# Moving the split of the first weight sum, and the two adding DMAs behind it, from the second product of a projection into the first

## The chip, the cores and the metric

The kernel runs on one core of a Trainium2 chip. A core has five engines that work side by side, each through its own instruction queue in order: TensorE (PE in the profile; its weight loads are listed as PEld) multiplies matrices, VectorE (DVE) and ScalarE (ACT) do elementwise work, GpSimd (POOL) and SyncE (SP) here mostly issue DMAs. Engines and DMAs wait for each other through semaphores. The metric is the time of one execution on the device in microseconds; a median over several executions is compared with that of another kernel.

## The reference

The reference is one decoder block on x of 1024 tokens by 1024 channels, in float32. What matters here is the middle of it:

```python
merged = (g_pool * jnp.einsum('bsc,cd->bsd', y_pool, w_branch_pool[l])
          + g_attn * jnp.einsum('bsc,cd->bsd', y_attn, w_branch_attn[l]))
mix = jnp.einsum('bsd,de->bse', merged, w_out[l])
x = x + _rmsnorm(mix, g_mix_post[l])
h2 = _rmsnorm(x, g_mlp_pre[l])
```

Before it stand a pooling branch, a windowed attention and two gates; after it a squared-ReLU MLP of 1024 to 4096 to 1024 channels and one more norm. The projection `merged @ w_out`, 1024 x 1024 by 1024 x 1024, is the part that the change touches.

## The kernel before, in words

**Precision.** Every float32 operand of a matmul is split into a high part (a cast to float32r on ScalarE, line 101) and a low part (the source minus the high part, on VectorE, line 104). A product is the sum of three matmul passes (high·high, high·low, low·high, the tuple `PASSES`).

**The projection.** It is computed as a 2 x 2 block product with seven block products instead of eight, each of 512 x 512 by 512 x 512. The four blocks of `w_out` are B11, B12, B21 and B22. The order of the products on TensorE is written out by hand: A11·B11, A12·B21 (into the same banks), S1·Q1, S2·Q2, S4·B22, S3·Q3, A22·Q4. S1 to S4 are sums of blocks of the activations. The weight sums are Q1 = B11 + B12, Q2 = Q1 + B22, Q4 = Q2 + B21 and Q3 = B12 + B22. Signs are arranged elsewhere so that only additions are needed.

**How the weight sums are made.** Q1, Q2 and Q4 live one after the other in the same buffers, `q1[0]` and `q1[1]` (128 x 1024 values each, 512 KB; two tiles of rows to each). SyncE loads B11 into them. Then GpSimd issues DMAs that read another block from DRAM and add it to what is in the buffer (`wo_add`, line 1000). Between two additions the current sum has to be split into its own high and low tiles (`wo_split`, which calls the helper of lines 101 and 104), since the next addition overwrites it. So the chain for each half is: add B12, split Q1, add B22, split Q2, add B21, split Q4. Q3 has buffers of its own (`q3`), with one addition. In the profile these buffers are named qr, the split tiles Q1h and Q1l, Q2h and Q2l and so on.

**How the order is set.** In this stage the order on TensorE, VectorE, ScalarE and GpSimd is that of the program text (`tc.manual_schedule`). `wo_mm` is a generator: it issues the 12 matmuls of one row tile (line 1089) and yields; the body of the loop around it then writes the work that follows that step, such as the copy of the finished bank on ScalarE. A product has four steps, 48 matmuls. The adding DMAs go through GpSimd's queue in program order: first two for q3, then two for q1 (B22), two for q1 (B21), and then those that accumulate output halves (line 1274) and write rows to DRAM (line 1127). SyncE's queue carries the plain loads: the weight blocks of the projection (line 995), the first weights of the MLP (line 483) and the rows of x for the residual (line 1120).

**The steps around the change.** In the first product, steps 0 and 1 split the two halves of B21, and each step copies its bank (line 1235 before the change). Between the first and second product the activation sums S1 and S2 are split (`s12`, named gr in the profile). In the second product each step copies its bank (line 1250) and adds an activation block (line 980), and steps 0 and 1 split Q1 and issue the addition of B22. After it B22 is split. In S1·Q1 each step copies its bank (line 1259); steps 0 and 1 split Q2 and issue the addition of B21. Behind the projection the finished rows are normed, added to x (lines 1123 and 1126), and transposed on TensorE (line 1135) for the MLP; some of these transposes stand between the matmuls of the last product.

Of the kernel before, what the change touches and what calls it, by code (L numbers as in the profile page):

```python
# [50 lines left out]
def block_kernel(ctx: ExitStack, tc, xt, x, consts, vecs, sinks, b_qkv, g_post, g_mlp, g_mlp_post,  # L51
# [16 lines left out]
    def nm(s):  # L68
        cnt[0] += 1
        return f"{s}_{cnt[0]}"  # L70
# [16 lines left out]
    def bank(tag, shape=None):  # L87
        return psum["pool"].tile([P] + (shape or [512]), F32, tag=tag, name=nm(tag), bufs=psum["bufs"][tag])
# [4 lines left out]
    def flat(t):  # L93
        return t.rearrange("p a b -> p (a b)")
# [4 lines left out]
    def split(hi, lo, src, eng=dve, first=None):  # L99
        if first is None:  # L100
            act.copy(hi, src)  # L101
        else:
            first.tensor_copy(hi, src)
        eng.tensor_tensor(lo, src, f32(hi), ALU.subtract)  # L104
# [732 lines left out]
    def gr(shape):  # L837
        return gp.tile([P] + shape, F32R, tag="g", name=nm("gr"))
# [116 lines left out]
    def flip(dst, src):  # L955
        act.activation(dst, src, AF.Identity, scale=-1.0)

    def split_half(tile_, src):
        t = tile_([2, 512])
        split(t[:, 0, :], t[:, 1, :], src)  # L960
        return t[:, 0, :], t[:, 1, :]

    def merged(m):
        zp = zm[m]
        first, second = zp[:, :512], zp[:, 512:]
        if m < 4:
            if m % 2 == 0:
                s3raw.append(ga_.tile([P, 2, 512], F32, tag="ga", name=nm("s3")))
            Am["A11"][m] = split_half(gr, first)
            dve.tensor_tensor(s3raw[m // 2][:, m % 2, :], first, second, ALU.subtract)  # L970
        else:
            k = m - 4
            s2, s1 = zm[k][:, :512], zm[k][:, 512:]
            Am["A12"][k] = split_half(ar, first)
            dve.tensor_tensor(s1, second, s1, ALU.subtract)
            dve.tensor_tensor(s2, s2, s1, ALU.add)

    def sum4(k):
        first = zm[4 + k][:, :512]
        dve.tensor_tensor(first, zm[k][:, :512], first, ALU.subtract)  # L980

    def wo_rows(c, h, j):
        return w_o[4 * h + 2 * c:4 * h + 2 * c + 2].rearrange("k p n -> p k n")[:, :, 512 * j:512 * j + 512]

    def wo_split(name, c, src, tile_):
        hi, lo = tile_(name + "h"), tile_(name + "l")
        split(hi, lo, flat(src))
        Wm.setdefault(name, [None] * 4)
        for i in range(2):
            Wm[name][2 * c + i] = hi[:, i * 512:(i + 1) * 512], lo[:, i * 512:(i + 1) * 512]  # L990

    def wo_raw(name, c, tile_):
        h, j = {"B11": (0, 0), "B12": (0, 1), "B21": (1, 0), "B22": (1, 1)}[name]
        t = tile_([2, 512])
        nc.sync.dma_start(t, wo_rows(c, h, j))
        return t

    def wo_add(t, name, c):
        h, j = {"B11": (0, 0), "B12": (0, 1), "B21": (1, 0), "B22": (1, 1)}[name]
        nc.gpsimd.dma_start(t, wo_rows(c, h, j), accum_op=ALU.add)  # L1000
# [18 lines left out]
    def bp_mul(m):  # L1019
        zp = gate_of.pop(m)  # L1020
        for th in range(2):
            sl = slice(th * 512, (th + 1) * 512)
            dve.tensor_tensor(zp[:, sl], zp[:, sl], bs_of[m][th], ALU.mult)
        dve.tensor_tensor(zp, zp, za[m], ALU.add)
        zm.append(zp)
# [4 lines left out]
    with tc.manual_schedule(engines=MANUAL):  # L1030
        q1 = [wo_raw("B11", c, wraw) for c in range(2)]
# [53 lines left out]
    def wo_mm(bs, a, w, after=False):  # L1085
        for t in range(4):
            for k in range(4):
                for j, (ah, wh) in enumerate(PASSES):
                    pe.matmul(bs[t], Am[a][k][ah][:, t * P:(t + 1) * P], Wm[w][k][wh],  # L1089
                              start=not after and k == 0 and j == 0, stop=k == 3 and j == 2, skip_group_check=after)  # L1090
            yield t
# [6 lines left out]
    def out_sq(n, h):  # L1098
        act.activation(junk_b[:, :512], ct[n][:, h * 512:(h + 1) * 512], AF.Square, scale=ROOT_D,
                       accum_out=osq[:, h, n:n + 1])  # L1100
# [121 lines left out]
    with tc.manual_schedule(engines=MANUAL):  # L1222
        bp_mul(7)
        bm = [bank("mm") for _ in range(4)]
        merged(7)
        q3 = [wo_raw("B12", c, wraw) for c in range(2)]
        for c in range(2):
            wo_add(q3[c], "B22", c)
        for t in wo_mm(bm, "A11", "B11"):
            if t == 0:  # L1230
                wo_split("B21", 0, b21[0], wo_tile)
            elif t == 1:
                wo_split("B21", 1, b21[1], wo_tile)
            ct[4 + t] = xq.tile([P, D], F32, tag="x1", name=nm("c2"))
            act.copy(ct[4 + t][:, :512], bm[t])
        flip(gpost_b[:, 512:], gpost_b[:, 512:])

        def s12(k):
            hi, lo = gr([D]), gr([D])
            split(hi, lo, zm[k])  # L1240
            Am["S2"][k] = hi[:, :512], lo[:, :512]
            Am["S1"][k] = hi[:, 512:], lo[:, 512:]

        b22 = [wo_raw("B22", c, stage) for c in range(2)]
        for k in range(4):
            s12(k)
        up.load(0)
        for t in wo_mm(bm, "A12", "B21", True):
            ct[t] = yy.tile([P, D], F32, tag="y", name=nm("c1"))
            act.copy(ct[t][:, :512], bm[t])  # L1250
            if t < 2:
                wo_split("Q1", t, q1[t], wo_tile)
                wo_add(q1[t], "B22", t)
            sum4(t)
        for c in range(2):
            wo_split("B22", c, b22[c], wo_tile)
        ba = [bank("at") for _ in range(4)]
        for t in wo_mm(ba, "S1", "Q1"):
            act.copy(ct[4 + t][:, 512:], ba[t])
            Am["A22"][t] = split_half(ar, zm[4 + t][:, 512:])  # L1260
            if t < 2:
                wo_split("Q2", t, q1[t], wo_tile)
                wo_add(q1[t], "B21", t)
            else:
                for k in (2 * t - 4, 2 * t - 3):
                    Am["S4"][k] = split_half(gr, zm[4 + k][:, :512])
        up.operand(0, 1)
        up.operand(0, 2)
        up.load(2)
        bm = [bank("mm") for _ in range(4)]  # L1270
        for t in wo_mm(bm, "S2", "Q2"):
            u = ct[4 + t]
            dve.tensor_tensor(u[:, :512], u[:, :512], bm[t], ALU.subtract)
            nc.gpsimd.dma_start(u[:, 512:], u[:, :512], accum_op=ALU.add)
            out_sq(t, 0)
            Am["S3"][t] = split_half(gr, s3raw[t // 2][:, t % 2, :])
            if t > 1:
                wo_split("Q3", t - 2, q3[t - 2], wo_tile)
# [478 lines left out]
```

## Time and profile before

| | us |
|---|---|
| median of 3 runs | 1108.01 |
| lowest and highest run | 1105.50 and 1108.25 |
| the profiled execution, its own time | 1107.79 |
| span of the profiled execution | 1106.0 |
| TensorE busy | 1095.2 (99% of the span) |
| VectorE busy | 822.8 (74%) |
| ScalarE busy | 551.8 (50%) |
| GpSimd busy | 54.2 (5%) |
| mean granted TensorE clock | 0.997 of full speed |

The projection lies between about 402 and 485 us of the span. Busy time of TensorE includes matmuls that run at a lower granted clock, so a share of 99% does not say that it runs at its fastest. A row of the timeline gives start, duration, engine, line, operation, output and inputs, and in square brackets the idle time of that engine before it and what ended it. Matmuls of 128 x 512 are pipelined: each has a duration of 0.39 us, but at full clock one starts every 0.227 us. Buffer numbers are left out of the names.

### The profile page before, as it was taken

Reading aid. Unit: us, or ns where it says so; the run is one execution under the profiler, and the core shown is the slowest. Engines: PE = TensorE matmul, PEld = TensorE weight load, DVE = VectorE, ACT = ScalarE, POOL = GpSimd, SP = SyncE. Lnnn points to the kernel's source line nnn. Section 1 sums busy time; section 2 is a strip of 40 time slices with the busy share of each in tenths; the row PEclk is TensorE's granted clock in tenths of the full one; section 3 lists DMA queues with packets and bytes.
Section 4 is the critical chain, followed back from the end, with each engine's and each line's share of the span. In section 5 each row is a group of like instructions: output and inputs, shape, how many; then the busy total and the mean of one; then the engine's idle time right before and its main releaser. Section 6 shows DMA issues by size and latency. Waiting matters only on the chain.

```text
span 1106.0 us, 13829 instructions
## 1 busy us (share of the span) xinstructions
PE 1095.2 (99%) x5114; PEld 909.4 (82%) x5114; DVE 822.8 (74%) x1179; ACT 551.8 (50%) x911; POOL 54.2 (5%) x112
## 2 busy tenths in 40 slices
PE   9999999999999999999999999999999999999997
PEld 8888888888888887888888888888888888888886
DVE  6568877898859777988978875756546875447797
ACT  7566665444332236566544544444436535435462
POOL 0334100000000001200000000000000000000000
PEclk9999999999999999999999999999999999999999
DMA  9614466365976564922455553435797876332652
GB/s 347 163 39 155 153 187 232 132 217 196 270 252 205 174 189 97 302 98 100 154 212 212 179 190 109 187 124 200 247 370 266 303 258 197 100 95 71 226 183 91
DMA packets 90803, 206.86 MB, mean 187 GB/s; under 512 B 9328, under 2 KB 22256, under 8 KB 90736
## 3 DMA queue, kind: packets, MB, share of 16 engines
q1 hardware_dynamic: 81072, 176.75, 47.6%
q10 hardware_dynamic: 5760, 19.79, 4.7%
q0 software_dynamic: 3904, 9.44, 3.8%
q8 instruction: 40, 0.66, 0.2%
q14 instruction: 27, 0.22, 0.1%
HBM read 149.32 MB, written 55.58 MB: 185 GB/s over the span
## 4 chain that ended last, share of the span: by engine, by line
PE 92%; DVE 3%; issue 2%; ACT 1%; DMA 1%; POOL 0%; DVEq 0%; POOLq 0%; ACTq 0%
PE mm L520 26%; PE at L520 16%; PE at L1525 15%; PE mm L1525 12%; PE mm L456 4%; PE mm L610 3%; PE mm L1089 3%; PE mm L458 2%; PE mm L192 2%; PE sc L183 2%; PE mm L183 2%; PE sc L429 1%; PE sc L360 1%; PE at L1089 1%; DMA qr<-in_w_o_dram 1%
## 5 line engine op out<-in xcount | busy, mean ns | idle before, releaser
L1525 PE MATMUL at<-ar,wh 128*128 128x512 f32 x696 | 158.7, 389 | 0.0
L1525 PEld LDWEIGHTS at<-ar,wh 128*128 128x128 f32 x696 | 130.6, 188 | 27.1
L1525 PE MATMUL mm<-ar,wh 128*128 128x512 f32 x576 | 131.0, 389 | 0.0
L1525 PEld LDWEIGHTS mm<-ar,wh 128*128 128x128 f32 x576 | 108.1, 188 | 22.5
L104 DVE TENSOR_TENSOR wh<-raw,wh 128x1024 fp32r<-128x1024 f32 x51 | 62.4, 1224 | 79.5 <-ACT wh L101 77.0
L101 ACT CAST wh<-st 128x512 fp32r<-128x512 f32 (+1 forms) x104 | 65.7, 641 | 95.6 <-DVE st L499 24.5
L101 ACT CAST wh<-raw 128x1024 fp32r<-128x1024 f32 x51 | 53.7, 1052 | 112.0 <-PE at L1525 55.4
L104 DVE TENSOR_TENSOR wh<-st,wh 128x512 fp32r<-128x512 f32 (+1 forms) x105 | 74.6, 720 | 30.2 <-ACT wh L101 27.6
L520 PE MATMUL mm<-gr,wh 128*128 128x512 f32 x333 | 79.4, 391 | 0.0
L520 PEld LDWEIGHTS mm<-gr,wh 128*128 128x128 f32 x333 | 62.1, 188 | 12.7
L520 PE MATMUL mm<-T,wx 128*128 128x512 f32 x288 | 67.4, 389 | 0.0
L520 PEld LDWEIGHTS mm<-T,wx 128*128 128x128 f32 x288 | 54.1, 188 | 11.2
L520 PE MATMUL at<-T,wx 128*128 128x512 f32 x252 | 58.9, 389 | 0.0
L520 PEld LDWEIGHTS at<-T,wx 128*128 128x128 f32 x252 | 47.3, 188 | 9.8
L520 PE MATMUL mm<-x,wh 128*128 128x512 f32 x240 | 55.2, 389 | 0.0
L520 PEld LDWEIGHTS mm<-x,wh 128*128 128x128 f32 x240 | 45.1, 188 | 9.3
L104 DVE TENSOR_TENSOR ar<-B,ar 128x1024 fp32r<-128x1024 f32 x37 | 45.2, 1221 | 5.6 <-ACT ar L101 5.5
L610 PE MATMUL mm<-x,wh 128*128 128x512 f32 x192 | 47.7, 395 | 0.0
L101 ACT CAST ar<-B 128x1024 fp32r<-128x1024 f32 x37 | 38.9, 1051 | 7.6 <-DMA B<-in_w_dn_dram 4.6
L610 PEld LDWEIGHTS mm<-x,wh 128*128 128x128 f32 x192 | 35.2, 188 | 7.5 <-DVE qt L104 0.2
L520 PE MATMUL at<-gr,wh 128*128 128x512 f32 x150 | 36.6, 390 | 0.0
L520 PE MATMUL mm<-T,wh 128*128 128x512 f32 x147 | 36.1, 389 | 0.0
(433 smaller groups left out, 2202.4 us busy)
## 6 DMA issues: line engine op xcount, KB each, us to landing
raw<-f_dram SPq DMA_DIRECT2D x53, 512.0 KB, 3.7
f_dram<-g SPq DMA_DIRECT2D x28, 512.0 KB, 3.0
st<-in_w_up_dram SPq DMA_DIRECT2D x24, 512.0 KB, 4.3
B<-in_w_dn_dram SPq DMA_DIRECT2D x24, 512.0 KB, 6.7
st<-in_w_g_dram SPq DMA_DIRECT2D x18, 512.0 KB, 3.9
f_dram<-g ACTq DMA_DIRECT2D x17, 512.0 KB, 3.4
g<-spill_dram SPq DMA_DIRECT2D x16, 512.0 KB, 4.9
raw<-in_w_dn_dram SPq DMA_DIRECT2D x16, 512.0 KB, 4.6
```

Of the source, the lines that this page charges most:

```text
L101: act.copy(hi, src)
L104: eng.tensor_tensor(lo, src, f32(hi), ALU.subtract)
L183: pe.matmul(bq, xs_[k][n // 4][:, xh, n % 4 * P:(n % 4 + 1) * P], wq[k][:, h, :], start=k == 0 and j == 0, stop=k == NK - 1 and j == 2)
L192: pe.matmul(bkv_of(n), xs_[k][n // 4][:, xh, n % 4 * P:(n % 4 + 1) * P], wkv[k // 2][:, h, k % 2, :], start=k == 0 and j == 0 and not (joi ...
L360: pe.matmul(sb[:, kv, i, :nk], qt[r, qx, m * P:(m + 1) * P], kx[r, k0:k0 + nk], start=j == 0, stop=j == 2)
L429: pe.matmul(yb[:, kv], v[:, c:c + P], p[ph][:, 4 * kv:4 * kv + 4].rearrange("p i q -> p (i q)"), start=j < 2, stop=j >= len(mms) - 2)
L456: pe.matmul(bs[th], whi[:, k, :], rhs(k, hl, th), start=k == 0 and hl == 0, stop=False)
L458: pe.matmul(bs[th], wlo[:, k, :], rhs(k, 0, th), start=False, stop=k == nk - 1)
L520: pe.matmul(b, w[:, wh, kt, :], x_, start=not after and kt == 0 and j == 0, stop=kt == 3 and j == 2, skip_group_check=after)
L610: pe.matmul(b, (whi, wlo)[h][:, k, :], xr(k, xh, th), start=j == 0, stop=j == len(mms) - 1)
L1089: pe.matmul(bs[t], Am[a][k][ah][:, t * P:(t + 1) * P], Wm[w][k][wh], start=not after and k == 0 and j == 0, stop=k == 3 and j == 2, skip_g ...
L1525: pe.matmul(bs[t], fo[fh][:, k2, t * P:(t + 1) * P], wo_[wh][:, k2, :], start=not after and s2 == 0 and k2 == 0 and j == 0, stop=(s2, k2) ...
```

## The change

The splits of Q1 move from steps 0 and 1 of the second product into steps 2 and 3 of the first one, ahead of the copy of the bank in those steps. The additions of B22 into q1 move with them and are issued directly behind each split. On GpSimd's queue the order of the DMAs stays; on ScalarE and VectorE the two casts and the two subtractions now stand ahead of the splits of S1 and S2. The instructions themselves stay the same.

```diff
--- before
+++ after
@@ -1231,6 +1231,9 @@
                 wo_split("B21", 0, b21[0], wo_tile)
             elif t == 1:
                 wo_split("B21", 1, b21[1], wo_tile)
+            else:
+                wo_split("Q1", t - 2, q1[t - 2], wo_tile)
+                wo_add(q1[t - 2], "B22", t - 2)
             ct[4 + t] = xq.tile([P, D], F32, tag="x1", name=nm("c2"))
             act.copy(ct[4 + t][:, :512], bm[t])
         flip(gpost_b[:, 512:], gpost_b[:, 512:])
@@ -1248,9 +1251,6 @@
         for t in wo_mm(bm, "A12", "B21", True):
             ct[t] = yy.tile([P, D], F32, tag="y", name=nm("c1"))
             act.copy(ct[t][:, :512], bm[t])
-            if t < 2:
-                wo_split("Q1", t, q1[t], wo_tile)
-                wo_add(q1[t], "B22", t)
             sum4(t)
         for c in range(2):
             wo_split("B22", c, b22[c], wo_tile)
```

## The prediction

> **What bounds the kernel now.** I read the chain of work that ended last, the waits of TensorE, then the order in time of each engine around the changed lines. The chain (shares of the span, by engine), the list of TensorE's waits, and one row of the chain in order of time:
>
> ```profile
> PE 92%; DVE 3%; issue 2%; ACT 1%; DMA 1%; POOL 0%; DVEq 0%; POOLq 0%; ACTq 0%
> ```
>
> ```profile
> PE mm L201 <- DVE pad L160: 1.1, 1, 1.1
> PE mm L1089 <- ACT Q2h L101: 1.0, 1, 1.0
> PE mm L1089 <- DVE Q2l L104: 0.8, 1, 0.8
> PE sc L403 <- DVE s L369: 0.5, 1, 0.5
> ```
>
> ```profile
> 449.46 10.88 PE at L1089 x48
> ```
>
> TensorE is the bound nearly everywhere, so only a change in its own gaps moves the end. These four waits are its whole list (total, times, longest), and two of them lie in the product S2·Q2, which this change is about. An undisturbed product of the projection is 48 matmuls in 10.88 us, 0.2267 us each. The product S2·Q2 starts at 434.43 and the product after it (operand B22) at 449.30 (start, duration, engine, line, operation):
>
> ```profile
> 434.43 0.39 PE L1089 MATMUL mm<-Q2h,gr 128*128 128x512 f32 x1
> ...
> 435.56 0.39 PE L1089 MATMUL mm<-Q2h,gr 128*128 128x512 f32 x1
> 436.98 0.50 PE L1089 MATMUL mm<-Q2h,gr 128*128 128x512 f32 x1 [1.02 <-ACT Q2h L101]
> 438.24 0.50 PE L1089 MATMUL mm<-Q2l,gr 128*128 128x512 f32 x1 [0.76 <-DVE Q2l L104]
> ...
> 449.30 0.39 PE L1089 MATMUL at<-B22h,gr 128*128 128x512 f32 x1
> ```
>
> That is 14.87 us, 3.99 us more than 10.88. The parts: the seventh matmul is due at 435.56 + 0.23 = 435.79 and comes at 436.98 (1.19 lost); the next is due at 437.21 and comes at 438.24 (1.03 lost); the remaining 1.77 us are lost after the waits, where the granted clock is down. The windows show this (length, then busy times of PE, PEld, DVE, ACT, POOL; then granted clock, DMA share, GB/s); the second row is the stretch around the 0.5 us wait of line 403:
>
> ```profile
> 439.30:442.90 3.60, 3.60 (x11) 2.79 (x10) 3.58 (x7) 3.60 (x9) 0.60 (x1) 0.53 0.56 100
> 112.00:116.00 4.00, 3.47 (x22) 2.85 (x21) 3.97 (x7) 1.73 (x4) 0.00 (x0) 1.00 0.99 291
> ```
>
> Eleven matmuls in 3.60 us at clock 0.53, where 16 would fit. A wait of 0.5 us elsewhere left the clock at 1.00; the two of S2·Q2 did not.
>
> **Why S2·Q2 waits.** Its second half of weights is q1[1] after the adding DMA of B22. GpSimd's queue of adding DMAs, and the time from issue to landing of the pair at 401 and 407, of the one at 427.13 and of the one at 442.30:
>
> ```profile
> 401.19 1.21 POOL L1000 DMA_DIRECT2D qr<-in_w_o_dram  x1 [39.82 <-DVE g L1024]
> 407.20 1.22 POOL L1000 DMA_DIRECT2D qr<-in_w_o_dram  x1 [4.81 <-issue]
> 421.13 1.21 POOL L1000 DMA_DIRECT2D qr<-in_w_o_dram  x1 [12.71 <-DVE Q1l L104]
> 427.13 1.21 POOL L1000 DMA_DIRECT2D qr<-in_w_o_dram  x1 [4.79 <-DMA qr<-in_w_o_dram]
> 436.12 1.21 POOL L1000 DMA_DIRECT2D qr<-in_w_o_dram  x1 [7.77 <-DMA qr<-in_w_o_dram]
> 442.30 1.22 POOL L1000 DMA_DIRECT2D qr<-in_w_o_dram  x1 [4.98 <-DVE gr L104]
> ```
>
> ```profile
> qr<-in_w_o_dram POOLq DMA_DIRECT2D x2, 512.0 KB, 5.8
> qr<-in_w_o_dram POOLq DMA_DIRECT2D x1, 512.0 KB, 8.7
> qr<-in_w_o_dram POOLq DMA_DIRECT2D x1, 512.0 KB, 9.1
> ```
>
> In these rows a second adding DMA of 512 KB never starts before the first has landed: the one of 421.13 is followed at 427.13, the one of 427.13 lands at 435.8 and is followed at 436.12. So a pair takes 6 us plus its second landing. The pair of Q2 starts at 421.13 because that is when the first low half of Q1 has been read (released by DVE Q1l). It ends at 435.8, 0.01 us after the seventh matmul was due, and cast (1.04) and subtraction (1.23) are still to come.
>
> **The change, part by part.** It moves two casts on ScalarE, two subtractions on VectorE and two adding DMAs of GpSimd from the second product into the third and fourth steps of the first; nothing is added or removed, and on SyncE's queue and on TensorE the order stays. ScalarE and VectorE before:
>
> ```profile
> 408.57 0.58 ACT L1235 COPY c<-mm 128x512 f32<-128x512 f32 x1
> 410.15 0.59 ACT L1235 COPY c<-mm 128x512 f32<-128x512 f32 x1 [1.00 <-PE mm L1089]
> 412.87 0.59 ACT L1235 COPY c<-mm 128x512 f32<-128x512 f32 x1 [2.13 <-PE mm L1089]
> ...
> 418.14 1.06 ACT L101 CAST Q1h<-qr 128x1024 fp32r<-128x1024 f32 x1
> ...
> 429.67 0.62 ACT L101 CAST ar<-g 128x512 fp32r<-128x512 f32 x1
> 435.88 1.04 ACT L101 CAST Q2h<-qr 128x1024 fp32r<-128x1024 f32 x1 [5.58 <-DMA qr<-in_w_o_dram]
> ```
>
> ```profile
> 408.26 2.36 DVE L104 TENSOR_TENSOR B21l<-st,B21h 128x1024 fp32r<-128x1024 f32 x2
> 414.95 4.63 DVE L104 TENSOR_TENSOR gr<-g,gr 128x1024 fp32r<-128x1024 f32 x4 [4.34 <-ACT gr L101]
> ...
> 436.96 1.23 DVE L104 TENSOR_TENSOR Q2l<-qr,Q2h 128x1024 fp32r<-128x1024 f32 x1 [5.94 <-ACT Q2h L101]
> ...
> 469.42 2.48 DVE L1126 SCALAR_TENSOR_TENSOR c<-g,r,c 128x1024 f32<-128x1024 f32 x2
> ```
>
> *Casts.* ScalarE stands idle 1.00 and 2.13 us ahead of the third and fourth copy. Two casts of 1.06 fit: 409.1 to 410.2, the third copy at 410.2 instead of 410.15, the second cast 410.7 to 411.8, the fourth copy unmoved at 412.87. The banks copied late are rewritten by the second product only at its third and fourth step, over 5 us later. Cost 0. If q1 were not there yet, ScalarE would stop in front of two copies and of the S1/S2 casts; but GpSimd was idle for 39.82 us before its add of 401.19, so the adds of B12 into q1 went out before 362.
>
> *Subtractions.* VectorE idles 4.34 us before 414.95; two of about 1.22 (the row of Q2l has the same shape) run from 410.6 to about 413.0. Cost 0. The casts and subtractions taken out of the second product leave holes there, worth nothing, since the copies around them wait for TensorE.
>
> *Adding DMAs.* They stand behind the q3 pair. Its second, of 407.20, lands at about 413.0, so the first of ours starts at 413.3 rather than at 411.8, where its own data would allow it. At 5.8 it lands at 419.1, at 9.1 at 422.4; the second starts 0.3 later and lands between 425.2 and 431.8. I take 426, near the short end, because the loads of SyncE that come next are these:
>
> ```profile
> 426.62 1.46 SPq L483 DMA_DIRECT2D st<-in_w_up_dram  x2
> ```
>
> The slow add of 427.13 ran beside them; ours are through or nearly so. The second cast of Q2 then follows the cast of 429.67 at 430.3, ends at 431.4, its subtraction at 432.6. TensorE wants them at 435.79 and 436.02. The margin is 3.4 us, and 1.8 us if the add lands at the late end. What is queued behind on GpSimd, the pair of B21 for Q4, goes out at about 430 instead of 436.12, and the adds of the output halves after it come earlier too.
>
> *Sum.* Both waits go (−1.19, −1.03). With no gap left there is nothing in the rows to bring the clock down, so −1.77 goes as well: −3.99 us. ScalarE and VectorE were held by the same DMA (5.58 and 5.94 us idle); without it they reach the work behind no later than the last result of S1·Q1, ready at about 434.6 when TensorE ends that product, so they keep up with it. The list of waits has nothing of TensorE's behind S2·Q2, and the loads there go to slots that come free with the shifted work; the shift reaches the end. Next in line is the first transpose of the normed rows:
>
> ```profile
> 473.79 1.03 PE L1135 MATMUL at<-cst,c 128*128 128x128 f32 x8
> ```
>
> The rows it reads are finished by the VectorE pair of 469.42, at 471.9: a margin of 1.9 us, which has to move along.
>
> The profiled execution took 1107.79 us for a span of 1106.0; 1107.79 − 3.99 = 1103.80. The median of the runs, 1108.01, is 0.22 above the profiled one, so the forecast stands about 4.2 us, 0.38%, under it.
>
> **The rivals.**
> *Only the waits go* (1107.79 − 2.22 = 1105.6). The slow clock could have come from something else than these gaps and stay. Against it: the window of 112 to 116 and the undisturbed products beside it run at 1.00, and the slow stretch begins 1 us after the second gap. For it: neither gap was longer than 1.2 us. The Trainium skill, TensorE: Matmul & The Clock Gate, Part 1, says that the clock is halved after at least one idle window of about 3.4 us; by that rule two gaps of 1.19 and 1.03 would not have done it, and this rival would hold. The trace has the half clock right behind them all the same. Chance 0.07.
>
> *The add lands late all the same; the change does nothing.* Were all of the three adds from 407.20 on to take 9.1 us, the last would land at 407.2 + 3 × 9.1 + 0.6 = 435.1, 0.7 us before now, and the time would be 1107.1. Of the landings above, one reached 9.1, one 8.7, and the pair that stands first in this queue took 5.8. Chance 0.04.
>
> *Given back at the transposes.* If the normed rows stay at 471.9 because their loads of x or VectorE's own chain do not move, TensorE, 4 us ahead at 469.8, waits 2.1 us: 1105.9, and with the clock falling again for 1.77, 1107.7. Against it: VectorE is worked through without a long wait from 437 on. Chance 0.08.
>
> *Slower, at the same place.* If an adding DMA or load of another 8.7 us gets in front of the x loads of these rows, because the GpSimd pair for Q4 and the SyncE loads of 426.62 now overlap, the rows come 8.7 us late: TensorE waits 8.7 − 1.9 = 6.8, plus 1.77 of clock, less 3.99: 1112.4. It decides from rows later than about 4.1 us against before. Against it: the Q4 pair, from 430 on, is then out of the way by 430 + 6.0 + 9.1 = 445, where now it lands at 442.3 + 9.1 = 451.4. Chance 0.07.
>
> **How the numbers follow.** The forecast has 0.74. A difference of 0.3% is 3.3 us, about what a measurement of this kernel tells from no change; the three runs alone lie 2.75 us apart, so 0.05 of the 0.74 may still measure less. Faster: 0.69. Within: 0.05 + 0.07 + 0.04 + 0.08 = 0.24. Slower: 0.07. The lower end of the range is the lowest run, 1105.5, less 3.99: 1101.5; the upper end takes in the late add and most of the given-back case, 1107.1.
>
> **What would show it.** The changed profile should have: the casts of Q1h near 409 and 411; adds issued near 413 and 419; no wait of TensorE for Q2h or Q2l; S2·Q2 in 10.88 us, clock 1.00; the B21 add near 430; the first transpose near 469.8 with no wait ahead of it. I am wrong if the second Q2 add lands after 433, if the slow clock shows up with no gap before it, or if TensorE waits at line 1135.

## The result, and the profile after

| | before | after |
|---|---|---|
| median, us (10 runs each, side by side) | 1108.12 | 1104.14 |
| lowest and highest, us | 1105.50 and 1109.08 | 1103.57 and 1105.36 |
| profiled execution: time and span, us | 1107.79 and 1106.0 | 1104.10 and 1102.3 |
| mean granted TensorE clock | 0.997 | 0.998 |

The ratio is 0.997, with a 95% interval of 0.996 to 0.998: faster by 0.3%, 3.98 us between the medians. The forecast was 1103.8.

The chain of the profile after, as shares by engine, and the whole list of TensorE's waits (total, times, longest):

```profile
PE 97%; DVE 2%; ACT 1%; issue 0%; DVEq 0%; ACTq 0%
```

```profile
PE mm L201 <- DVE pad L160: 1.1, 1, 1.1
PE sc L403 <- DVE s L369: 0.5, 1, 0.5
```

The DMA's 1% and the 2% of issue time are gone from the chain: before, it ran back from the wait for Q2 through GpSimd's queue, now it stays on TensorE there. These shares are not time saved. Both waits for Q2 are gone from the list. The chain in order of time (start, duration, what) shows S2·Q2, in the banks named mm, and the B22 product behind it; then the window of S2·Q2 (length, busy times of PE, PEld, DVE, ACT, POOL, then the granted clock, DMA share, GB/s):

```profile
434.57 10.88 PE mm L1089 x48
445.45 10.88 PE at L1089 x48
```

```profile
434.20:445.10 10.90, 10.90 (x50) 9.03 (x49) 8.64 (x14) 9.62 (x20) 3.85 (x4) 1.00 0.75 162
```

S2·Q2 takes 10.88 us at clock 1.00. The B22 product stood at 449.46 in the chain before and stands at 445.45 now: 4.01 us earlier. GpSimd's queue after (start, duration, engine, line, operation, and the idle time before it), then the landing times of the two that feed Q2:

```profile
402.06 1.21 POOL L1000 DMA_DIRECT2D qr<-in_w_o_dram  x1 [42.08 <-PE mm L458]
407.97 1.22 POOL L1000 DMA_DIRECT2D qr<-in_w_o_dram  x1 [4.71 <-PE mm L1089]
414.17 1.21 POOL L1000 DMA_DIRECT2D qr<-in_w_o_dram  x1 [4.98 <-issue]
420.06 1.21 POOL L1000 DMA_DIRECT2D qr<-in_w_o_dram  x1 [4.68 <-DMA qr<-in_w_o_dram]
430.18 1.21 POOL L1000 DMA_DIRECT2D qr<-in_w_o_dram  x1 [8.90 <-DVE Q2l L104]
436.39 1.22 POOL L1000 DMA_DIRECT2D qr<-in_w_o_dram  x1 [5.00 <-issue]
```

```profile
qr<-in_w_o_dram POOLq DMA_DIRECT2D x1, 512.0 KB, 5.6
qr<-in_w_o_dram POOLq DMA_DIRECT2D x1, 512.0 KB, 5.9
```

The pair for Q2 now follows the q3 pair at the pitch of this queue, about 6 us, and the second of it has landed at 420.06 + 5.9 = 426.0, before SyncE's loads of 426.6 begin. Before, it was issued at 427.13. ScalarE and VectorE:

```profile
409.01 1.06 ACT L101 CAST Q1h<-qr 128x1024 fp32r<-128x1024 f32 x1
410.13 0.59 ACT L1238 COPY c<-mm 128x512 f32<-128x512 f32 x1
410.61 1.05 ACT L101 CAST Q1h<-qr 128x1024 fp32r<-128x1024 f32 x1
412.85 0.59 ACT L1238 COPY c<-mm 128x512 f32<-128x512 f32 x1 [1.18 <-PE mm L1089]
...
430.17 1.05 ACT L101 CAST Q2h<-qr 128x1024 fp32r<-128x1024 f32 x1
```

```profile
410.49 2.43 DVE L104 TENSOR_TENSOR Q1l<-qr,Q1h 128x1024 fp32r<-128x1024 f32 x2
414.93 4.63 DVE L104 TENSOR_TENSOR gr<-g,gr 128x1024 fp32r<-128x1024 f32 x4 [2.01 <-ACT gr L101]
...
431.25 1.23 DVE L104 TENSOR_TENSOR Q2l<-qr,Q2h 128x1024 fp32r<-128x1024 f32 x1 [0.26 <-ACT Q2h L101]
465.40 2.48 DVE L1126 SCALAR_TENSOR_TENSOR c<-g,r,c 128x1024 f32<-128x1024 f32 x2
```

```profile
469.77 1.03 PE L1135 MATMUL at<-cst,c 128*128 128x128 f32 x8
```

The casts and subtractions lie in what was idle time; the bank copies behind them moved by no more than 0.02 us (410.13 and 412.85, against 410.15 and 412.87). The last Q2 low half is ready at 432.48; the first transpose starts at 469.77, 4.02 us earlier than before.

Of these 4.0 us, 3.7 reach the end. The last stretch of the MLP's second product shows where 0.3 stayed (chain in order of time, the profile before and then the one after), with the weight-load wait after:

```profile
1055.01 31.29 PE at L1525 x138
```

```profile
1051.00 31.58 PE at L1525 x138
```

```profile
PEld at L1525 <- DVE hold L104: 0.4, 1, 0.4
```

The same 138 matmuls take 0.29 us more, behind a wait for a split of other data (hold). Whether the change causes that is looked at below.

### The profile page after: what moved, and what is told of

Read it like the earlier page. It is cut to its first block, busy times and chain, and to the rows that moved or that the text cites. A ratio compares the mean times of both kernels' runs of the same rounds, so it can differ in the third digit from the quotient of the medians.

```text
span 1102.3 us, 13829 instructions
## 1 busy us (share of the span) xinstructions
PE 1093.3 (99%) x5114; PEld 908.9 (82%) x5114; DVE 822.7 (75%) x1179; ACT 552.1 (50%) x911; POOL 54.1 (5%) x112
## 4 chain that ended last, share of the span: by engine, by line
PE 97%; DVE 2%; ACT 1%; issue 0%; DVEq 0%; ACTq 0%
PE mm L520 26%; PE at L520 16%; PE at L1525 15%; PE mm L1525 12%; PE mm L456 5%; PE mm L1089 5%; PE mm L610 3%; PE mm L458 3%; PE mm L192 2%; PE sc L183 2%; PE mm L183 2%; PE at L1089 2%; PE sc L429 1%; PE sc L360 1%; PE at L1135 1%; PE sc L403 1%
```

## The experiments

The theory is that of the prediction: S2·Q2 waited for the second adding DMA of B22, and the half clock was a consequence of the two waits. The rivals that had to be told apart: the waits go but the half clock has another cause; the place of the casts and subtractions matters, not that of the DMAs; a rule of the queue other than its room for one transfer sets the 6 us pitch.

**Half the way: splits and additions after the third split of S1 and S2.** The pair starts later than in the changed kernel, but a little earlier than before.

```diff
         for k in range(4):
             s12(k)
+            if k == 2:
+                for t in range(2):
+                    wo_split("Q1", t, q1[t], wo_tile)
+                    wo_add(q1[t], "B22", t)
 ...
             act.copy(ct[t][:, :512], bm[t])
-            if t < 2:
-                wo_split("Q1", t, q1[t], wo_tile)
-                wo_add(q1[t], "B22", t)
             sum4(t)
```

> The splits of Q1 and their two adds stand between the third and the fourth split of S1/S2, so the low half of Q1 is ready 1.1 us earlier than before. My theory: the adds go out near 420.0 and 426.0 instead of 421.13 and 427.13, the late one lands near 434.7 if it again takes 8.7 us, the cast of Q2 just makes 435.8 and TensorE has one wait of about 1.1 us, for the low half. S2 x Q2 takes 10.88 + 1.1 = 12.0 us if one wait of that length leaves the clock alone (time 1105.2 where before is 1108.1), and 13.7 us if any wait over 1 us brings the half clock (1107.0). Rival, that the clock drop is not tied to the wait and that the changed kernel only happened to miss it: a slow stretch of 3.6 us stays, wherever it falls, whatever the wait is. Rival, that the gain of the change came from emptying the second product on ScalarE and VectorE: full gain of 4.0 us is not reached by moving the adds 1.1 us, but neither is any change of the wait seen, 1108.

Measured: 1105.57 us, ratio 0.9976 (0.9967 to 0.9985). TensorE's row behind its one wait for Q2, and the window of S2·Q2:

```profile
437.74 0.50 PE L1089 MATMUL mm<-Q2l,gr 128*128 128x512 f32 x1 [0.76 <-DVE Q2l L104]
```

```profile
435.10:447.20 12.10, 11.34 (x49) 8.94 (x49) 10.73 (x16) 11.83 (x25) 3.34 (x3) 1.00 0.55 101
```

The second add was issued at 426.93 and landed 8.4 us later, at 435.3: half a microsecond before the 435.8 of the kernel before. That took away the first wait and left the second, 1.01 us from when the matmul was due. The product took 12.06 us, and the clock stayed at 1.00. So behind one gap of 1 us there is no half clock here; the 1.8 us of slow clock went when one of the two waits went. All ten executions of this version were granted a mean clock of 0.998 or 0.999.

**Only the second half moved.** Its split and its addition go to the last step of the first product, ahead of those of the first half, which stay where they were.

```diff
             elif t == 1:
                 wo_split("B21", 1, b21[1], wo_tile)
+            elif t == 3:
+                wo_split("Q1", 1, q1[1], wo_tile)
+                wo_add(q1[1], "B22", 1)
 ...
-            if t < 2:
+            if t == 0:
                 wo_split("Q1", t, q1[t], wo_tile)
                 wo_add(q1[t], "B22", t)
```

> Only half of the change: the split of the second half of Q1 and its add move into step 3 of the first product, ahead of the other half on GpSimd; the first half stays in step 0 of the second product. My theory: adds near 414 (second half) and 421.1 (first half, by 427 as before), no add has another of its pair in front of it, so neither cast of Q2 waits. S2 x Q2 in 10.88 us, 1104.1. Rival, that both splits have to be out of the second product: some of the wait of before stays, 1106 to 1108.

Measured: 1105.19 us, ratio 0.9973 (0.996 to 0.9985). The adds went out at 414.11 and 421.19, the second cast of Q2 ran at 430.24, and the chain has S2·Q2 undisturbed:

```profile
434.64 10.88 PE mm L1089 x48
```

It is enough that one add of the pair leaves when the q3 pair is through. The first half's split at its old place costs nothing in this trace. Nine of the ten runs lie between 1103.95 and 1105.87; the tenth took 1109.76, and no trace shows why.

**The order of before, with room for two additions.** The program's parameter `dynamic_dma_scratch_size`, taken here as the room for the descriptors (the prepared orders) of DMAs that GpSimd issues, is doubled; no instruction moves.

```diff
-    nc = bacc.Bacc("TRN2", target_bir_lowering=False, num_devices=1, dynamic_dma_scratch_size=1024)
+    nc = bacc.Bacc("TRN2", target_bir_lowering=False, num_devices=1, dynamic_dma_scratch_size=2048)
```

> The kernel before with one number changed: GpSimd's space for prepared DMAs is doubled; no instruction moves on any engine. My theory says that the second add of a pair waits for the first to land because both do not fit. Then the second add of the pair at 421 goes out 1.2 to 2 us behind the first instead of 6.0, lands by about 431, TensorE does not wait in S2 x Q2 (10.88 us) and the time is near 1104.1 with the order of before. Rival, that GpSimd itself takes 6 us to prepare an add of 512 KB: the adds stay 6.0 us apart and the time stays at 1108.1.

Measured: 1104.80 us, ratio 0.9971 (0.9958 to 0.9983). GpSimd's rows of the Q2 pair:

```profile
421.24 1.21 POOL L1000 DMA_DIRECT2D qr<-in_w_o_dram  x1 [17.35 <-DVE Q1l L104]
422.98 1.20 POOL L1000 DMA_DIRECT2D qr<-in_w_o_dram  x1 [0.53 <-DVE Q1l L104]
```

The second add leaves 1.74 us behind the first, as soon as its own data is free; before, it left 6.0 us behind, when the first had landed. S2·Q2 takes 10.88 us, with no wait for Q2. This settles two things: the 6 us pitch came from the room that this parameter gives, and the place of the casts and subtractions is not what the gain hangs on, since here they did not move. The Trainium skill, DMA: Bandwidth & Descriptors, section SWDGE vs HWDGE vs iDMA, says that GpSimd writes the descriptors of its DMAs into rings kept in a reserved part of SBUF. That the parameter sets the size of that part is our reading; that changing it changes the pitch, 1.74 us against 6.0, agrees with it.

**Both additions held back.** They wait behind a small GpSimd copy of the bank of the second product's last step. The first version gave the copy a tile of its own:

```diff
             if t < 2:
                 wo_split("Q1", t, q1[t], wo_tile)
-                wo_add(q1[t], "B22", t)
+            if t == 3:
+                hold_pool = small(8, "hp")
+                pool.tensor_copy(hold_pool, ct[t][:, :8])
+                for c in range(2):
+                    wo_add(q1[c], "B22", c)
             sum4(t)
```

> The kernel before, but the two adds of B22 stand behind a copy of 128 x 8 values on GpSimd that waits for the last bank copy of the second product (about 424.4), so they go out near 424.8 and 430.8, 3.7 us later than before; the splits stay where they were. My theory: S2 x Q2 waits longer by as much as the second add lands later. At 8.7 us to landing, 439.5, the waits are 4.9 and 1.0 us; at 5.9, since the loads of 426.6 are through by then, 436.7, the waits are 2.1 and 1.0. With 1.8 us of half clock the product takes 15.8 to 18.6 us and the time is 1109.0 to 1111.8. Rival, that the time of the adds does not matter and the place of the splits does: no change, 1108.1. Rival, clock independent of waits: the same longer waits but no slow stretch, or one elsewhere.

Measured: 1127.61 us, ratio 1.0167 (1.0151 to 1.0183). That was a miss. S2·Q2 took 15.77 us against 14.87, which is 0.9 of the 20; but matmuls far away from the change had slowed down too: 192 of them in the MLP take 44.80 us where they took 43.52. The suspicion was that the new tile had moved the addresses of others. So the delay was made again with no new tile (the copy writes into `orr`, an existing tile), and the shift of addresses was made alone.

```diff
             if t < 2:
                 wo_split("Q1", t, q1[t], wo_tile)
-                wo_add(q1[t], "B22", t)
+            if t == 3:
+                pool.tensor_copy(orr, ct[t][:, :NT])
+                for c in range(2):
+                    wo_add(q1[c], "B22", c)
             sum4(t)
```

> The delay of the adds again, with GpSimd's copy writing into a tile that is there already (orr, which is filled anew later), so that no address moves. My theory: the adds go out near 424.8 and 430.8, the second lands near 436.7, the cast of Q2 ends 2.1 us and its subtraction 3.2 us after TensorE wants them; with 1.8 us of half clock S2 x Q2 takes 15.9 us and the time is about 1109.1, 5 us over the changed kernel. If the second add lands late again, at 8.7 us, 1111.8. Rival, that the place of the splits and not the time of the adds made the gain: 1108.1 as before, with S2 x Q2 at 14.9.

Measured: 1111.18 us, ratio 1.0024 (1.001 to 1.0038). The adds went out at 426.09 and 432.29, the second 5.2 us later than before. TensorE's rows behind its two waits, and the window behind the first of them:

```profile
439.36 0.79 PE L1089 MATMUL mm<-Q2h,gr 128*128 128x512 f32 x1 [2.38 <-ACT Q2h L101]
440.62 0.79 PE L1089 MATMUL mm<-Q2l,gr 128*128 128x512 f32 x1 [0.47 <-DVE Q2l L104]
```

```profile
439.40:446.00 6.60, 6.13 (x14) 4.46 (x15) 6.58 (x10) 6.60 (x15) 1.53 (x2) 0.51 0.50 79
```

S2·Q2 took 17.09 us, from 435.46 to 452.55: 10.88, plus 2.54 and 1.03 lost at the waits (against the times at which the matmuls were due), plus 2.64 of half clock. A later add makes the kernel slower through the same waits that the change removes. The expectation had 15.9 us and 1109.1: the adds left 1.3 and 1.5 us later than it had them, and the part of the clock is not a constant 1.8, since the stretch at half clock lasted 6.83 us here and 3.41 before (the clock records of the traces). That the time is near the expectation's other price, 1111.8, is luck: that one was for a second add that takes 8.7 us to land, and this one took 5.9. The ten executions spread from 1107.48 to 1113.01. The 192 matmuls in the MLP take 43.52 us, as before.

**Only the addresses.** The kernel before with one small tile enlarged by 96 bytes per partition, and twice more with 128 and 64 (its 32 values become 56, 64 and 48):

```diff
-    pad = sp.tile([P, 32], F32, name="pad", bufs=1)
+    pad = sp.tile([P, 56], F32, name="pad", bufs=1)
```

> The kernel before with one tile made larger: the constant tile pad of 32 values per partition has 56, so every SBUF tile allocated after it moves by 96 bytes; no instruction moves. The delayed adds of the earlier run came with a new small tile of the same 96 bytes and with matmuls 0.2333 us apart instead of 0.2267 in the whole kernel. Theory that the addresses did that: matmul spacing 0.233 here too, time near 1127 although nothing of the order is changed. Rival, that GpSimd's copy or the later adds slowed TensorE: spacing 0.2267 and 1108.

> The kernel before with the tile pad at 64 values per partition, so that all SBUF tiles behind it move by 128 bytes. If what cost 17 us at 96 bytes is the offset from a round address, 128 keeps it: matmul spacing 0.2267 and 1108. If any move of the tiles against the tiles in front of them costs it: 0.233 and 1125.

> The same with 48 values, a move of 64 bytes. By the offset theory 1108 if multiples of 64 bytes are enough, 1125 if the round address is coarser than that.

Measured: 96 bytes, 1124.71 us, ratio 1.0153 (1.0135 to 1.0171); 128 bytes, 1125.04, and 64 bytes, 1115.94, one run each. The largest group of matmuls of the MLP's products (count, then busy us and mean ns of one, then idle time before them), in the kernel before and with 96, 128 and 64 bytes more:

```profile
L1525 PE MATMUL at<-ar,wh 128*128 128x512 f32 x696 | 158.7, 389 | 0.0
```

```profile
L1525 PE MATMUL at<-ar,wh 128*128 128x512 f32 x696 | 163.4, 395 | 0.0
```

```profile
L1525 PE MATMUL at<-ar,wh 128*128 128x512 f32 x696 | 163.4, 395 | 0.0
```

```profile
L1525 PE MATMUL at<-ar,wh 128*128 128x512 f32 x696 | 160.3, 391 | 0.0
```

So the first delayed version owed most of its 20 us to the addresses: the shift alone costs 17. It also means that it says little about the change, and the second one stands in its place. That a distance from a round address decides is not borne out, since 128 bytes cost as much as 96. What does decide stays open.

These versions keep the order of before, and so they show its two waits again. With 64 bytes more, TensorE's rows behind the two waits, and the window behind the second:

```profile
439.62 0.51 PE L1089 MATMUL mm<-Q2h,gr 128*128 128x512 f32 x1 [1.28 <-ACT Q2h L101]
440.88 0.50 PE L1089 MATMUL mm<-Q2l,gr 128*128 128x512 f32 x1 [0.76 <-DVE Q2l L104]
```

```profile
440.90:444.50 3.60, 3.60 (x16) 2.91 (x17) 3.58 (x7) 3.60 (x8) 0.00 (x0) 1.00 0.84 137
```

Against the times at which the matmuls were due, 1.44 and 1.03 us are lost here, more than the 1.19 and 1.03 of the kernel before, and the clock stays at 1.00. With 96 and 128 bytes more, 1.54 and 1.82 are lost at the first wait and 1.03 at the second, and the clock is at 0.50 behind them. So two gaps of this length do not always bring the half clock.

**The two kernels once more,** unedited, one run each, for the scatter of the margin and of the 0.3 us at the end.

> The kernel before, unchanged, for a second profile. Theory: S2 x Q2 again near 14.9 us with two waits of about 1.2 and 1.0 and some 3.5 us at half clock. Open: whether TensorE waits for the last operand tiles of the down product (hold), which it did for 0.3 to 0.8 us in four profiles of other kernels and not in the first profile of this one. If it does here, the 0.3 us that the changed kernel fell short of 3.99 is scatter of that place; if it never does, the change itself brought it.

> The changed kernel, unchanged, for a second profile. Theory: S2 x Q2 10.88 us, no wait and no slow clock there, span 1102 to 1103; the wait for the last operand tiles anywhere from 0 to 0.8 us.

Measured: 1108.65 us and 1104.54 us. The kernel before had S2·Q2 in 14.79 us, again with both waits (1.0 and 0.8 in the list) and a stretch at clock 0.50. It also had this wait at the end of the MLP, which its first profile did not have:

```profile
PE at L1525 <- DVE hold L104: 0.5, 1, 0.5
```

So that wait comes and goes without the change, and the 0.3 us by which the span fell short of 4.0 lies within the scatter of that place. The changed kernel, again, GpSimd's rows of the Q2 pair and the second cast of Q2:

```profile
417.38 1.21 POOL L1000 DMA_DIRECT2D qr<-in_w_o_dram  x1 [7.34 <-DVE gr L104]
424.71 1.21 POOL L1000 DMA_DIRECT2D qr<-in_w_o_dram  x1 [6.12 <-DMA qr<-in_w_o_dram]
```

```profile
430.38 1.05 ACT L101 CAST Q2h<-qr 128x1024 fp32r<-128x1024 f32 x1 [0.34 <-DMA qr<-in_w_o_dram]
```

The second add left 4.65 us later than in the first profile, and yet the cast is only 0.21 us later and S2·Q2 still takes 10.88: the cast had stood behind other work of ScalarE until 430.17 anyway. Most of that lateness fell into slack that the first profile had not shown as such: the add may land up to about 430 without moving anything.

**Both together:** the changed kernel with the doubled reservation.

```diff
-    nc = bacc.Bacc("TRN2", target_bir_lowering=False, num_devices=1, dynamic_dma_scratch_size=1024)
+    nc = bacc.Bacc("TRN2", target_bir_lowering=False, num_devices=1, dynamic_dma_scratch_size=2048)
```

> The changed kernel with GpSimd's space for prepared DMAs doubled as well. Theory: each of the two alone takes TensorE's wait in S2 x Q2 away, so together they give nothing more: 1104 to 1105, with the second add of each pair 1.3 to 2 us behind the first. Rival, that one of them leaves a rest of the wait which the profile does not show: 1102 to 1103.

Measured: 1105.53 us, ratio to the kernel before 0.9974 (0.9962 to 0.9986), which overlaps the 0.996 to 0.998 of the change alone. The pair goes out together at 411.68, and S2·Q2 takes the same 10.88. Once TensorE does not wait for Q2, an earlier Q2 is worth nothing. None of the versions here beats the changed kernel.

## Why the prediction was right

*What S2·Q2 waits for.* It was the second add, as the prediction said. An add that lands 0.5 us earlier (1105.57 us), one that lands in time without any move (1104.80), and one that leaves 5.2 us later (1111.18) move the time in the direction and in the order that this step asks for.

*The queue never starts a second add of 512 KB before the first has landed.* Right as an observation, and doubling the descriptor space ended it: the cause was the room that the parameter gives, not the transfers themselves, nor 6 us that GpSimd would need to prepare an add.

*Casts and subtractions at cost 0.* Right: the casts at 409.01 and 410.61 and the subtractions at 410.49 fall within 0.1 us of the places given, and the copies did not move.

*Adding DMAs near 413.3 and 419.4, landed by about 426.* They left at 414.17 and 420.06 and the second landed at 426.0. The first was 0.9 us late, because the q3 pair itself was 0.8 us later in this profile (407.97 against 407.20). The margin at the low half was 3.5 us: the matmul that wants it starts at 436.00, and it was ready at 432.48. The forecast was 3.4. The repeat shows that the choice of the short landing time was not something to rely on: there the pair came 3 to 5 us later. The outcome did not hang on it.

*Half clock as a consequence of the two waits (−1.77).* Right for the two profiled executions: without gaps the window is at 1.00, and the rival "only the waits go" has fallen, since all ten runs of the changed kernel lie under its 1105.6. It is not right as a rule. By the clock records of the thirteen traces, the granted clock changes in each of them only at times a whole number of 3.41 us apart. In slices between such times, TensorE (by its rows) was idle for 1.62 us of the one from 436.11 to 439.52 in the kernel before, and for 1.73 in its repeat, and the clock was halved for the slice behind. In the 64-byte version the edge at 438.92 divides the first gap; the slice behind the edge has 1.46 us idle, the one ahead 0.58, and the clock stays at 1.00. Over all the traces, a slice at full clock with 1.73 us or more idle was always followed by half clock and one with 1.46 or less never; in between, 1.62 was, and 1.69 was not (at the end of the run with both changes). So where the gaps fall decides as well as how long they are. The Trainium skill, TensorE: Matmul & The Clock Gate, Part 1, has the clock halved after an idle window of about 3.4 us. The length of the slices agrees with that; that the whole of it would have to be idle does not, by the 1.62 and 1.73 us, and the measurement decides here. How idle time is weighed within a slice is not known from these runs.

By an estimate, only some executions of the kernel before had the slow stretch. A slice at half clock takes 0.0015 off the mean clock, and the half clock behind the last matmul at least 0.001 more in every trace, which leaves 0.997; of the 48 executions of the kernel before that were run beside the experiments, 32 were granted 0.998 or 0.999. Their mean is 1107.4 us, that of the other 16 1109.4. The term of 1.77 was taken from an execution that had the stretch.

*The sum, −3.99.* 4.01 us at the product behind S2·Q2, 4.02 at the first transpose, 3.7 in the span of the one profile, 3.98 between the medians. For the two profiles the sum is right term by term. That the medians agree so closely is in part luck: the three other medians of the kernel before, 1107.37 to 1108.41, stand 3.2 to 4.3 us over 1104.14. The 32 executions without the stretch stand 3.3 over it, more than the 2.22 of the two waits; how long their waits were, no trace shows.

*Given back at the transposes.* It did not happen. The rows are finished at 465.40 + 2.48 = 467.88 and read at 469.77: the margin of 1.9 us moved along whole.

*Slower at the same place.* The two transfers of the Q4 pair left at 430.18 and 436.39, and no load got in their way at a cost: the list of TensorE's matmul waits has nothing behind S2·Q2.

## What to carry to other kernels

Before a DMA is moved, look at what its queue lets it start behind: here the second of two additions waited 6 us for the landing of the first, so the time of the pair was set by when the pair's first one left. A short gap on the bounding engine can cost more than its length: in the profiled execution two waits of 1 us were worth 4, in others less by the estimate above, so such a term is better taken from more than one execution. And when a small tile is added for an experiment, compare the spacing of matmuls far from it, or the experiment measures the addresses.

## What the runs showed of the hardware that was not expected

Moving SBUF tiles by 64, 96 or 128 bytes per partition slowed matmuls all through the MLP, with no wait and no lower clock to be seen: from 43.52 us for 192 to 43.95, 44.80 and 44.80 (0.2267 us each to 0.2289 and 0.2333), 8 to 17 us of the whole.

The granted clock changed only at times a whole number of 3.41 us apart, so a slow stretch had one of few lengths: 3.41 us after first gaps of 1.1 to 1.9 us and second ones of 1.03 (both profiles of the kernel before, the first delayed version, 96 and 128 bytes more), 6.83 us after 2.54 and 1.03, and none after 1.44 and 1.03 that such a time divided.
